# A row softmax on one core: the loads of tiles two to six issued from GpSimd, each DMA engine's share in one packet

## The chip, the core and the metric

The kernel runs on one core of a Trainium2 chip. A core has engines that each follow their own list of instructions: VectorE (DVE), ScalarE (ACT), GpSimd (POOL), SyncE (SP) and TensorE, which this kernel doesn't use. Data moves between the chip's main memory (HBM) and the core's on-chip memory (SBUF, 128 partitions) by 16 DMA engines. An engine of the core issues a transfer into a DMA queue; the DMA engines carry it out. The metric is the time of one execution on the device in microseconds, lower being better.

## What is computed

The input has 16 x 1024 = 16,384 rows of 512 float32 values, 33.55 MB; the output has the same size. Each row gets a softmax at temperature 0.5:

```python
x_scaled = x / 0.5
x_max = np.max(x_scaled, axis=-1, keepdims=True)
exp_x = np.exp(x_scaled - x_max)
return exp_x / np.sum(exp_x, axis=-1, keepdims=True)
```

## The kernel before

The 16,384 rows are cut into 8 tiles of 2048 rows, 4 MiB each. In a tile every partition holds 16 rows that lie side by side in HBM, so it gets 32 KB in one contiguous piece. There are six buffers: tiles one to six (c = 0 to 5 in the code) have one each, and tiles seven and eight take those of tiles one and two again once these are stored. All work is done in place in the buffer.

A tile is worked on in blocks of rows. The first tile has blocks of 4, 4 and 8 rows, the last has two of 8, all others are one block of 16. Its loads are cut too: the first tile arrives as two transfers, of 4 rows (8 KB in a partition, 1 MiB in all) and of 12 rows (24 KB, 3 MiB); each other tile is one transfer.

For a block, `shift` (line 68) takes each row's negated maximum on VectorE (line 74) and doubles it to a bias (line 78). `exponentials` (line 80) runs one ScalarE instruction for each row, exp(2x + bias), which sums the row as it goes (line 85). `scale_vector` (line 95) forms reciprocals (line 100) and multiplies seven eighths of the rows by them on VectorE (line 102); `scale_scalar` (line 106) does the rest on ScalarE (line 111). `store` (line 115) sends a whole tile out from ScalarE's queue after its last block (line 119).

The order is written by hand, at lines 123 to 133: the maximum of block i + 2 comes after the scaling of block i, and the exponentials of block i + 1 ahead of it. So VectorE's list takes the tiles strictly in their order, and no later tile's work can go ahead of an earlier tile's. The loads are issued by `load` (line 59), which `shift` calls at the first touch of a tile; all are issued on Sync (line 66). Sync does nothing else. The first six tiles' loads wait for nothing, as their buffers are new; the seventh's waits, among others, for the first tile's store, and the eighth's for the second's. All loads therefore stand in one queue, in the order of the tiles.

Of the kernel before, what the change touches and what calls it, by code (L numbers as in the profile page):

```python
# [1 line left out]

# [4 lines left out]


@with_exitstack
def kernel(  # L10
    ctx: ExitStack,
    tc: tile.TileContext,
    x: bass.AP,
    out: bass.AP,
):
    nc = tc.nc
    fp32 = mybir.dt.float32
    P = nc.NUM_PARTITIONS
    AX = mybir.AxisListType.X
    EXP = mybir.ActivationFunctionType.Exp  # L20
    COPY = mybir.ActivationFunctionType.Copy
    MAX = mybir.AluOpType.max

    D = x.shape[-1]
    xf = x.flatten_outer_dims()
    of = out.flatten_outer_dims()
    N = xf.shape[0]

    G = 16
    C = N // (P * G)
    assert C * P * G == N
    xr = xf.rearrange("(c p g) d -> c p g d", p=P, g=G)
    outr = of.rearrange("(c p g) d -> c p g d", p=P, g=G)
    WHOLE = [(0, G)]
    LOADS = [[(0, 4), (4, G)]] + [WHOLE] * 7
    BLOCKS = [[(0, 4), (4, 8), (8, G)]] + [WHOLE] * 6 + [[(0, 8), (8, G)]]
    STORES = [WHOLE] * 8  # L40
    BMAX = 16
    BUFS = 6

    data = ctx.enter_context(tc.tile_pool(name="data", bufs=BUFS))
    stats = ctx.enter_context(tc.tile_pool(name="stats", bufs=6))

    ctx.enter_context(tc.manual_schedule())


    warm = stats.tile([P, 1], fp32, name="warm", bufs=1)  # L50
    nc.vector.memset(warm, 0.0)  # L51
    nc.scalar.activation(out=warm, in_=warm, func=EXP)  # L52

    chunks = {}
    blocks = [(c, lo, hi) for c in range(C) for lo, hi in BLOCKS[c]]
    n = len(blocks)
    biases, sums, recips = {}, {}, {}

    def load(c):
        if c < BUFS:  # L60
            chunks[c] = data.tile([P, G, D], fp32, name="xt")
        else:
            chunks[c] = chunks[c - BUFS]
        xt = chunks[c]
        for lo, hi in LOADS[c]:
            nc.sync.dma_start(out=xt[:, lo:hi, :], in_=xr[c][:, lo:hi, :])  # L66

    def shift(i):
        c, lo, hi = blocks[i]
        if c not in chunks:  # L70
            load(c)
        b = hi - lo
        negmax = stats.tile([P, BMAX], fp32, name="negmax")
        nc.vector.tensor_reduce(  # L74
            negmax[:, 0:b], chunks[c][:, lo:hi, :], axis=AX, op=MAX, negate=True
        )
        biases[i] = stats.tile([P, BMAX], fp32, name="bias")
        nc.vector.tensor_scalar_mul(biases[i][:, 0:b], negmax[:, 0:b], 2.0)  # L78

    def exponentials(i):  # L80
        c, lo, hi = blocks[i]
        sums[i] = stats.tile([P, BMAX], fp32, name="sums")
        for g in range(hi - lo):
            row = chunks[c][:, lo + g, :]
            nc.scalar.activation(  # L85
                out=row,
                in_=row,
                func=EXP,
                bias=biases[i][:, g : g + 1],
                scale=2.0,  # L90
                accum_out=sums[i][:, g : g + 1],
            )


    def scale_vector(i):
        c, lo, hi = blocks[i]
        b = hi - lo
        k = b - b // 8
        recips[i] = stats.tile([P, BMAX], fp32, name="recip")
        nc.vector.reciprocal(recips[i][:, 0:b], sums[i][:, 0:b])  # L100
        rows = chunks[c][:, lo : lo + k, :]
        nc.vector.tensor_mul(  # L102
            rows, rows, recips[i][:, 0:k].unsqueeze(2).broadcast_to((P, k, D))
        )

    def scale_scalar(i):
        c, lo, hi = blocks[i]
        b = hi - lo
        for g in range(b - b // 8, b):
            row = chunks[c][:, lo + g, :]  # L110
            nc.scalar.activation(  # L111
                out=row, in_=row, func=COPY, scale=recips[i][:, g : g + 1]
            )

    def store(i):
        c, _, end = blocks[i]
        for lo, hi in STORES[c]:
            if hi == end:
                nc.scalar.dma_start(
                    out=outr[c][:, lo:hi, :], in_=chunks[c][:, lo:hi, :]  # L120
                )

    shift(0)
    shift(1)
    exponentials(0)
    for i in range(n):
        if i + 1 < n:
            exponentials(i + 1)
        scale_vector(i)
        scale_scalar(i)  # L130
        if i + 2 < n:
            shift(i + 2)
        store(i)


# [1 line left out]
_INS = ['x']  # L137
_OUTS = [((16, 1024, 512), 'float32')]


# [23 lines left out]
```

## Time and profile before

| What | Value |
|---|---|
| Time, median of 3 runs | 162.28 us (162.20 to 162.33) |
| The profiled execution: its time / its span | 162.34 us / 160.6 us |
| VectorE busy | 134.6 us, 84% of the span |
| ScalarE busy | 102.1 us, 64% |
| GpSimd busy | 0.2 us, four small fills at the start |
| Bytes moved | 67.13 MB, 418 GB/s over the span |
| Landing of a load after its issue | 4.9 us (first piece), 11.7 us (second piece), 30.2 us (median of the whole tiles) |
| Landing of a store after its issue | 12.2 us shortest, 22.8 us median |

The span is the time from the first to the last thing that the profile records; the time of the execution has 1.7 us around it. A landing counts from the issue, so a load that stands behind others in its queue has their transfer in its own figure. The page's strip of DMA activity, 40 slices of the span, says how full the 16 DMA engines were:

```profile
DMA  5999999999999999999999999999999999999993
GB/s 182 471 400 506 400 400 498 408 392 484 424 400 384 400 457 449 400 441 465 400 424 473 408 408 492 400 392 498 416 392 490 424 392 457 457 392 449 465 392 139
```

Each digit is the busy share in tenths, 9 for 90% or more. The row of VectorE on the page looks much the same from the fourth slice to the 37th: both resources are nearly full through the middle of the run.

### The profile page before, as it was taken

The page shows a single profiled execution, that of the slowest core. Times are in us where ns is not written, and L with a number is a line of the kernel's source. Part 1 is how long each engine was busy: PE and PEld are TensorE (multiplying, and loading weights), DVE is VectorE, ACT ScalarE, POOL GpSimd, SP SyncE. Part 2 cuts the span into 40 slices and gives each one's busy share as a digit, 9 for nine tenths or more (in the row PEclk, how much of TensorE's full clock was granted, in tenths as well). Part 3 has the DMA queues.
Part 4 walks back from the last instruction along what each step waited for, and adds up shares of the span by engine and source line. Part 5 has one row for each costly group of instructions (what it writes and reads, how often), then busy time and mean ns, then how long its engine had stood idle before and what let it go on. Part 6 is the DMA issues. An engine that isn't in the chain of part 4 may idle for free.

```text
span 160.6 us, 402 instructions
## 1 busy us (share of the span) xinstructions
DVE 134.6 (84%) x45; ACT 102.1 (64%) x273; POOL 0.2 (0%) x4
## 2 busy tenths in 40 slices
DVE  0507999999999999999999999999999999957000
ACT  3071549069979963998199909991899891790000
POOL 0000000000000000000000000000000000000000
DMA  5999999999999999999999999999999999999993
GB/s 182 471 400 506 400 400 498 408 392 484 424 400 384 400 457 449 400 441 465 400 424 473 408 408 492 400 392 498 416 392 490 424 392 457 457 392 449 465 392 139
DMA packets 2450, 67.13 MB, mean 418 GB/s; under 512 B 272, under 2 KB 272, under 8 KB 272
## 3 DMA queue, kind: packets, MB, share of 16 engines
q1 hardware_dynamic: 1296, 33.56, 49.3%
q10 hardware_dynamic: 1152, 33.55, 48.4%
q14 instruction: 2, 0.02, 0.0%
HBM read 33.55 MB, written 33.55 MB: 418 GB/s over the span
## 4 chain that ended last, share of the span: by engine, by line
DVE 80%; DMA 7%; ACT 4%; issue 0%; SPq 0%
DVE negmax L74 42%; DVE xt L102 36%; DMA xt<-in_x_dram 7%; ACT xt L85 4%; DVE bias L78 1%; DVE recip L100 1%; SPq L66 0%
## 5 line engine op out<-in xcount | busy, mean ns | idle before, releaser
L85 ACT ACTIVATE xt<-xt,bias 128x512 f32<-128x512 f32 x128 | 90.4, 708 | 41.7 <-DVE bias L78 41.2
L74 DVE TENSOR_REDUCE negmax<-xt 128x16 f32<-128x8192 f32 (+2 forms) x11 | 69.9, 6352 | 9.5 <-DMA xt<-in_x_dram 9.5
L102 DVE TENSOR_TENSOR xt<-xt,recip 128x7168 f32<-128x7168 f32 (+2 forms) x11 | 62.0, 5637 | 0.4
L85 ACT ACTIVATION_READ_ACCUMULATOR xt<-xt,bias 128x1 f32 x128 | 23.9, 187 | 0.0
L111 ACT ACTIVATE xt<-xt,recip 128x512 f32<-128x512 f32 x15 | 9.9, 706 | 0.0
L100 DVE RECIPROCAL recip<-sums 128x16 f32<-128x16 f32 (+2 forms) x11 | 2.4, 218 | 1.8 <-ACT xt L85 1.8
L78 DVE TENSOR_SCALAR bias<-negmax 128x16 f32<-128x16 f32 (+2 forms) x11 | 1.9, 173 | 0.4
L52 ACT ACT_TABLE_LOAD x1 | 1.3, 1283 | 0.7 <-PEq L148 0.7
L51 DVE MEMSET warm<- 128x1 f32 x1 | 0.1, 59 | 0.8 <-PEq L148 0.8
L52 ACT ACTIVATE warm<-warm 128x1 f32<-128x1 f32 x1 | 0.2, 203 | 0.0
L148 POOL MEMSET const-bfloat16-1.0<- 128x1 bf16 x1 | 0.1, 103 | 0.0
L148 POOL MEMSET const-uint8-127<- 128x1 uint8 x1 | 0.1, 103 | 0.0
L148 POOL MEMSET const-float32-1.0<- 128x1 f32 x1 | 0.1, 100 | 0.0
L148 POOL MEMSET const-float32-0.0<- 128x1 f32 x1 | 0.1, 99 | 0.2 <-issue 0.2
## 6 DMA issues: line engine op xcount, KB each, us to landing
out_dram<-xt ACTq DMA_DIRECT2D x8, 4096.0 KB, 22.8
xt<-in_x_dram SPq DMA_DIRECT2D x7, 4096.0 KB, 30.2
xt<-in_x_dram SPq DMA_DIRECT2D x1, 3072.0 KB, 11.7
xt<-in_x_dram SPq DMA_DIRECT2D x1, 1024.0 KB, 4.9
```

What stands on the lines that cost most here:

```text
L51: nc.vector.memset(warm, 0.0)
L52: nc.scalar.activation(out=warm, in_=warm, func=EXP)
L74: nc.vector.tensor_reduce(negmax[:, 0:b], chunks[c][:, lo:hi, :], axis=AX, op=MAX, negate=True)
L78: nc.vector.tensor_scalar_mul(biases[i][:, 0:b], negmax[:, 0:b], 2.0)
L85: nc.scalar.activation(out=row, in_=row, func=EXP, bias=biases[i][:, g : g + 1], scale=2.0, accum_out=sums[i][:, g : g + 1],)
L100: nc.vector.reciprocal(recips[i][:, 0:b], sums[i][:, 0:b])
L102: nc.vector.tensor_mul(rows, rows, recips[i][:, 0:k].unsqueeze(2).broadcast_to((P, k, D)))
L111: nc.scalar.activation(out=row, in_=row, func=COPY, scale=recips[i][:, g : g + 1])
L148: nc = _bacc.Bacc("TRN2", target_bir_lowering=False, num_devices=1)
```

## The change

Loads of tiles two to six, those with 0 < c < 6, are issued on GpSimd. A transfer is handed to the DMA engines as descriptors, records of which bytes to move, here one for each 32 KB piece; packets are what the DMA engines work through. The argument single_packet asks that what one DMA engine has of a transfer, here 8 pieces of 32 KB, be put into one packet. The two transfers of the first tile and the loads of tiles seven and eight stay on Sync. In the changed code Sync's list is four loads, GpSimd's five; the lists of VectorE and ScalarE are the same as before.

```diff
         for lo, hi in LOADS[c]:
-            nc.sync.dma_start(out=xt[:, lo:hi, :], in_=xr[c][:, lo:hi, :])
+
+            if 0 < c < BUFS:
+                nc.gpsimd.dma_start(
+                    out=xt[:, lo:hi, :], in_=xr[c][:, lo:hi, :], single_packet=True
+                )
+            else:
+                nc.sync.dma_start(out=xt[:, lo:hi, :], in_=xr[c][:, lo:hi, :])
```

## The prediction

> **What bounds the kernel now.** I read the chain of waits first, because it says whether the loads or the arithmetic set the end. Its columns are start in us, length in us, and what.
>
> ```profile
> by line: DVE negmax L74 41.7%; DVE xt L102 36.2%; DMA xt<-in_x_dram 7.3%; ACT xt L85 3.6%; DVE bias L78 1.1%; DVE recip L100 0.9%; issue 0.4%; SPq L66 0.2%
> 1.15 11.71 DMA xt<-in_x_dram
> 12.86 0.02 issue
> 12.88 2.30 DVE negmax L74
> ...
> 143.59 3.89 DVE xt L102
> ```
>
> The chain has one DMA piece, the load of rows 4 to 15 of the first tile, landing at 12.86. From 12.88 VectorE is the chain up to 147.5, but for 5.76 us of ScalarE near the end. So the rest of the span hangs on that landing: 160.6 - 12.86 = 147.7 us follow it whatever happens ahead.
>
> Next, the list of waits, to see where VectorE starves:
>
> ```profile
> DVE negmax L74 <- DMA xt<-in_x_dram: 9.5, 2, 4.8
> ```
>
> It waited for loads twice only, for the two pieces of the first tile. Tiles two to eight were always there in time. The load of the second tile is needed only at 24.63.
>
> Then the table of busy time by stretch (length, VectorE, ScalarE, GpSimd, clock, DMA share, GB/s):
>
> ```profile
> 2.50:5.60 3.10, 0.00 (x0) 0.00 (x0) 0.00 (x0) 1.00 1.01 423
> 5.60:12.90 7.30, 2.48 (x3) 2.93 (x8) 0.00 (x0) 1.00 1.03 446
> 12.90:45.60 32.70, 32.49 (x13) 20.68 (x57) 0.00 (x0) 1.00 1.00 433
> 45.60:59.00 13.40, 13.33 (x5) 12.61 (x34) 0.00 (x0) 1.00 1.01 411
> ```
>
> The DMA engines are full from 2.5 us on, during the first tile's load too: bytes put ahead of that tile delay it one for one. Between 12.9 and 45.6 only loads move, at 433 GB/s, or 27.06 GB/s for each of 16 engines. I price all loads with this.
>
> Last, the DMA view of the time in which loads (q1) and the first store (q10) compete, 46 to 69 us:
>
> ```profile
> q1 hardware_dynamic: 186, 5.57, 59.5%
> q10 hardware_dynamic: 144, 4.19, 42.2%
> ```
>
> Shares of packet time add to 101.7%: an engine serves one packet at a time, and the two queues take turns. With 32 KB in each packet, 5.57 MB are 170 packets and 4.19 MB are 128, so the load queue got 1.33 packets for one of the store queue.
>
> **What the Trainium skill says.** In "DMA: Bandwidth & Descriptors", section "Queues, rings and completion order", each DMA engine goes round its queues at packet granularity: it "drains a whole packet" from one before it switches. The turns above agree, but no run here yet shows a packet with several descriptors. The section "SWDGE vs HWDGE vs iDMA" of that page prefers packets of up to 4096 B and at most 64 descriptors, and calls the packet the context-switching boundary; GpSimd's queue and Sync's are different queues of an engine. The section "The descriptor swizzle" counts eight data descriptors and one completion for each engine of a 128-partition transfer; the page's 1296 packets of the load queue are 9 loads x 16 engines x 9, in agreement. In "Latency and other measured facts" the first byte takes about 0.6 us from Sync and about 1 us from GpSimd. The trace has the first Sync issue at 0.73 and packets from about 1.7 us; GpSimd's figure no run here shows.
>
> **The change part by part.** Order and number of instructions on VectorE and ScalarE are unchanged. Sync loses five load issues, GpSimd gains five, and nothing on GpSimd waits ahead of them.
>
> 1. Removed from Sync: five issues of 0.42 to 0.65 us. In the trace they follow the two issues of the first tile and nobody waits for their issue time, so the gain is nothing. The loads of the seventh and eighth tile wait for stores in any case (56.4 us the longest wait on Sync), and nothing stands between them that the change moves.
>
> 2. Added on GpSimd: five issues, on an engine idle after 0.43 us. It isn't shown how long one takes. By the skill's 1 us the first tile-2 descriptors are at the DMA engines near 0.7 + 1 = 1.7 us (an estimate); I take 2.5 us, and bound it by 1.7 and, for a slow start, 7 us. VectorE is idle up to 5.61, so it can't be in the way of the first ones. By 2.5 us Sync's queue has moved 19 packets, about one for each engine, of the 16 data packets (8 of 8 KB, 8 of 24 KB) an engine has for the first tile.
>
> 3. The packets. In each GpSimd load an engine has 8 x 32 KB = 262,144 B, and with single_packet that is one packet. At 27.06 GB/s a share holds the engine for 262,144 / 27.06e3 = 9.69 us. Sync's packets of the first tile hold it for 0.31 or 0.91 us. Taking turns then means: a Sync packet or 1.33, a share of 9.69 us, a Sync packet or 1.33, the next share, and so on. Before, the first tile stood ahead of all others in one queue; now all five are ahead of most of it. There are five shares, and five turns let through only 5 x 1.33 = 6.7 of about 15 Sync packets. So all five shares go by before the last Sync packet, on every engine. This holds for any start of GpSimd up to when 6.7 Sync packets are left: 12.86 - 6.7 x 0.91 = 6.8 us.
>
> 4. The cost. The second piece of the first tile lands later by 5 x 9.69 = 48.4 us, at 61.3 instead of 12.86. What hides it? Nothing: VectorE has only the first block (2.29 + 0.17 us) to do before, and the second tile, although landed early, comes after the first in VectorE's order. The first piece (8 KB packets) is late as well, by up to five shares, but lands some 7 us (8 packets of 0.91) ahead of the second, which covers its 2.46 us on VectorE and four exponentials on ScalarE.
>
> 5. Afterwards. All of tiles one to six are in place when VectorE starts, so its 134.6 us run as before. The first store goes out at 45.58 + 48.4 = 94.0 with no load beside it; it took 23.7 us in competition and 12.2 alone (the shortest landing of a store). Tile seven's load can start near 106 and is needed at 103.94 + 48.4 = 152.3: no new wait. The DMA engines have more idle time later, which buys nothing, since VectorE doesn't wait there. The last store lands as before, about 12.2 us after its issue.
>
> 6. A GpSimd queue to close at the end may add a little: between 0 and about 0.5 us, an estimate by the size of one issue; I take 0.
>
> Sum: the profiled execution took 162.34 us, of which the span is 160.6 and 1.7 lie around it. 160.6 + 48.4 = 209.0 of span, 210.7 us in all; its own time stands 0.06 above the median of 162.28, so against the median it is the same. I write 210.5.
>
> In general the time is 162.3 + 9.69 k, where k is the number of GpSimd shares (or their equal in bytes) that pass before the last Sync packet of the first tile. The rivals are values of k.
>
> **Rivals.**
> - Turns by descriptor: the DMA engine switches after each 32 KB, as it does between loads and stores. Then about 14 Sync packets at 1.33 to 1 let 10.5 to 14 descriptors of 1.21 us in between: 12.7 to 17 us, so 175 to 179 us. For it speaks that each descriptor of 32 KB is one packet of the record before; against it, that the change asks for one packet.
> - Only a few shares ahead: the engine already holds most of the first tile's packets when GpSimd's arrive, or shares bandwidth by bytes. One share is 172.0, equal bytes (240 KB, 8.9 us) 171.2, three shares 191. For it: Sync issues both pieces by 1.6 us. Against it: the two queues of before do take turns while both have work queued long before.
> - The other side: GpSimd's first descriptors reach the DMA engines only after the first tile has gone, at 12.86 or later. Then the queue order is that of before, tile two has until 24.63, and the time is 162.3; with less traffic behind it the first tile might land up to 0.5 us earlier (4.19 MB at 433 GB/s are 9.7 us from 1.7, that is 11.4, plus the slow start), so 161.8 to 162.5. It would need 12 us between barrier and first packet on an otherwise idle engine; nothing in the profile speaks for so much. Beyond 12.86 + about 2 us tile two would itself be late, which is slower again.
>
> **How the numbers follow.** All five shares ahead: 0.55, from 205 to 214 (the loads at 411 GB/s, the rate of 45.6 to 59, would make 51.0 us of the 48.4, so 213.3). By descriptor: 0.17. A few shares or equal bytes: 0.11. GpSimd late: 0.13, of it 0.09 no change and 0.04 faster. Still slower than 214, by GpSimd loads that run below the rate of Sync's: 0.04. Differences within 0.2% (0.3 us) count as none. The range from 171 to 214 takes in the first three; the likeliest case alone has 205 to 214. Slower is 0.55 + 0.17 + 0.11 + 0.04 = 0.87.
>
> **What would show it.** Right: VectorE's wait for loads grows from 9.5 to about 58 us, the chain's DMA piece ends near 61, GpSimd's queue moves 20.97 MB nearly all before the first tile's last packet, and from there the chain repeats that of before shifted by 48 us. By-descriptor turns would put the landing at 25 to 30 and a mix of both queues in that time. A first GpSimd packet after 12.9, with the landing at 12.86, would make the forecast wrong altogether; a landing in between gives k. If VectorE waits for loads again after the first tile, step 5 is wrong.

## The result, and the profile after

The changed kernel takes 171.26 us (median of 4 runs, 171.25 to 171.29), the kernel before 162.24: a ratio of 1.0556, 95% interval 1.0538 to 1.0575. It is 9 us slower. The forecast was slower too, but by 48 us. Of all the runs in this document one is left out of the comparisons, because it took over 1.5% longer than the fastest of its kernel: 192.97 us of e3_desc8k_no_single.

The chain of waits after (start in us, length, what), to be held against the one of before:

```profile
by line: DVE negmax L80 39.5%; DVE xt L108 34.3%; DMA xt<-in_x_dram 12.6%; ACT xt L91 3.4%; DVE bias L84 1.0%; DVE recip L106 0.9%; issue 0.4%; SPq L72 0.2%
...
1.16 21.35 DMA xt<-in_x_dram
22.54 2.30 DVE negmax L80
...
153.25 3.89 DVE xt L108
```

The shape is that of before. The one DMA piece, the second piece of the first tile, ends at 1.16 + 21.35 = 22.51 instead of 12.86, 9.65 us later, and VectorE's last instruction starts at 153.25 instead of 143.59, 9.66 us later. Everything between is carried along unchanged. The list of waits says the same, and shows no new wait:

```profile
DVE negmax L80 <- DMA xt<-in_x_dram: 19.2, 2, 14.5
```

VectorE waits for loads twice, as before, for 19.2 us instead of 9.5.

So the place was as forecast, and the size was not. The DMA view of the stretch from 6.8 to 21.6 us shows why (queue, packets, MB, share of the 16 engines; q0 is GpSimd's queue, q1 Sync's):

```profile
DMA packets 224, 6.42 MB, mean 434 GB/s; under 512 B 0, under 2 KB 0, under 8 KB 0
## 3 DMA queue, kind: packets, MB, share of 16 engines
q0 software_dynamic: 112, 3.67, 57.4%
q1 hardware_dynamic: 112, 2.75, 43.1%
```

112 and 112: seven from each queue on each of 16 engines, one of 32 KB from GpSimd and one of 24 KB from Sync in turn. A share, the eight descriptors that one DMA engine has of a load, does not go through as a unit. The record counts each descriptor as a packet on GpSimd's queue as well, although the transfer was issued with single_packet.

Where GpSimd begins is seen in the list by time (start, length, engine, line, in brackets the idle time before) and in the DMA view from 1.2 to 5.55 us. The list:

```profile
1.24 2.75 POOL L68 DMA_DIRECT2D xt<-in_x_dram  x5 [0.79 <-PEq L165]
```

The DMA view of that stretch has one queue:

```profile
q1 hardware_dynamic: 160, 1.44, 88.8%
```

GpSimd has issued all five loads by 4.0, but up to 5.55 only Sync's queue moves data. GpSimd's first 16 descriptors start between 5.59 and 6.10. By then each engine has moved the first piece and one packet of the second, which is why the first piece still lands in 4.8 us. What is left on each engine is seven packets and the small write that reports completion. Each of these eight lets one descriptor by. The DMA view from 5 to 21.62 us, when the first completions of the second piece are written, counts them:

```profile
q0 software_dynamic: 128, 4.19, 58.4%
```

128 on 16 engines are 8 on each. By the packets' recorded durations one takes 1.213 us; 8 x 1.213 = 9.70 us, against 9.65 measured.

The span grew by 8.9 us, not 9.65. Before, the last store took 12.16 us to land, since the preceding store still had data in the queue (164 packets in the last 13.1 us, where one store is 144). Now it lands in 11.13 us. The end of the span follows the landing by 1.13 us instead of 0.85, which takes 0.28 of this back.

### The profile page after: what moved, and what is told of

It reads as the page before. It is cut to its first block, busy times and chain, and to the rows that moved or that the text cites. A ratio compares the mean times of both kernels' runs of the same rounds, so it can differ in the third digit from the quotient of the medians.

```text
span 169.5 us, 404 instructions
## 1 busy us (share of the span) xinstructions
DVE 134.6 (79%) x45; ACT 102.3 (60%) x273; POOL 3.0 (2%) x9
## 4 chain that ended last, share of the span: by engine, by line
DVE 76%; DMA 13%; ACT 3%; issue 0%; SPq 0%
DVE negmax L80 40%; DVE xt L108 34%; DMA xt<-in_x_dram 13%; ACT xt L91 3%; DVE bias L84 1%; DVE recip L106 1%; SPq L72 0%
## 5 line engine op out<-in xcount | busy, mean ns | idle before, releaser
L80 DVE TENSOR_REDUCE negmax<-xt 128x16 f32<-128x8192 f32 (+2 forms) x11 | 69.9, 6353 | 19.2 <-DMA xt<-in_x_dram 19.2
L68 POOL DMA_DIRECT2D xt<-in_x_dram x5 | 2.8, 557 | 0.8 <-PEq L165 0.8
## 6 DMA issues: line engine op xcount, KB each, us to landing
xt<-in_x_dram POOLq DMA_DIRECT2D x5, 4096.0 KB, 39.5
```

The costliest lines, as they stand in the source:

```text
L68: nc.gpsimd.dma_start(out=xt[:, lo:hi, :], in_=xr[c][:, lo:hi, :], single_packet=True)
L80: nc.vector.tensor_reduce(negmax[:, 0:b], chunks[c][:, lo:hi, :], axis=AX, op=MAX, negate=True)
```

## The experiments

Theory T: a DMA engine that has work in several queues takes one descriptor from each in turn, whatever single_packet says. A transfer with n descriptors left on an engine is therefore delayed by n times the length of the other queue's descriptor. The main rivals were that a whole share, but only one, gets ahead (9.69 us, the same size by chance); that turns are equal in bytes; that GpSimd's path has a price of its own; and that the price is in proportion to what is moved to GpSimd. All diffs are against the changed kernel unless something else is said.

**Without the argument (e1_no_single)**

```diff
-                    out=xt[:, lo:hi, :], in_=xr[c][:, lo:hi, :], single_packet=True
+                    out=xt[:, lo:hi, :], in_=xr[c][:, lo:hi, :]
```

> The changed kernel without single_packet. Theory T (a DMA engine changes queues after every descriptor, whatever packet it belongs to): nothing changes, 171.3 us within 0.3, the second piece of the first tile lands at 22.5 again. Rival R (the argument does shape the turns, and only about one share got ahead): without it the turns should be other than now, with a landing clearly before or after 22.5 and a time at least 1 us away from 171.3.

Measured: 171.28 us, landing at 22.47. For descriptors of 32 KB the argument makes no difference.

**Short descriptors on GpSimd (e2_desc8k, e3_desc8k_no_single)**

```diff
-                    out=xt[:, lo:hi, :], in_=xr[c][:, lo:hi, :], single_packet=True
+                    out=xt[:, lo:hi, :], in_=xr[c][:, lo:hi, :], single_packet=True,
+                    max_dma_last_dim=8192
```

The second of the two has max_dma_last_dim in place of single_packet.

> The changed kernel with GpSimd's descriptors cut from 32 KB to 8 KB, still single_packet, so a share is 32 descriptors in one packet. Theory T: each of the 8 turns given to GpSimd now costs 0.31 us instead of 1.21, so the delay is about 8 x 0.31 = 2.5 us and the time 164 to 165. Rivals: one whole share ahead of Sync's packets, or turns equal in bytes, leave the delay at 8 to 9.7 us, 170 to 171.5.

> As e2_desc8k but without single_packet. Theory T: the same as e2_desc8k within 0.3 us. Rival R: the two differ by more than 1 us, since 32 descriptors to a packet or 1 is then a large difference.

Measured: 191.65 us and, for the three runs of e3_desc8k_no_single that are compared, 189.05 us. The time is far from every expectation, but the landing is T's. The chain of waits of e2_desc8k:

```profile
1.15 14.31 DMA xt<-in_x_dram
15.48 2.30 DVE negmax L81
...
90.01 27.31 another core or an unknown queue
117.34 8.70 DVE negmax L81
```

The second piece lands at 15.46, 2.60 us later than before; T said 2.5. One share ahead, or turns equal in bytes, would have been 8 to 9.7. What follows is a wait that no theory had: VectorE stands still for 27.31 us until 117.34. The chain can't name it; the list of waits puts it down to a load ("DVE negmax L81 <- DMA xt<-in_x_dram: 39.5, 3, 27.3"), and it is the sixth tile's, GpSimd's last. The DMA view from 70 to 110 us explains it:

```profile
q1 hardware_dynamic: 252, 7.73, 44.9%
q10 hardware_dynamic: 257, 7.37, 42.7%
q0 software_dynamic: 259, 2.11, 12.5%
```

Three queues, Sync's loads of tiles seven and eight (q1), the stores (q10) and GpSimd's loads (q0), get the same number of packets, 252 to 259. With 32 KB in those of the first two and 8 KB in GpSimd's, GpSimd's loads have an eighth of the engines. Short descriptors made them harmless to the first tile, and then starved the sixth, by the same rule.

The two kernels are not equal, as T had it within 0.3 us. The four runs of e2_desc8k lie between 191.31 and 193.41, the three of e3_desc8k_no_single between 188.95 and 190.00; their medians are 2.6 us apart, more than the 1 us that rival R asked for. It is weak evidence for R all the same. The first tile lands alike in both, at 15.46 and 15.35, and from 70 to 110 us the three queues get equal counts without single_packet too (255, 256 and 260). In that stretch a DMA engine gets to one of GpSimd's descriptors about every 2.5 us (259 on 16 engines in 40 us). So one descriptor more or less on the slowest engine is worth about 2.5 us (an estimate). In the profiled runs, 1.6 us apart, the difference is one descriptor: of GpSimd's 2560 the last starts at 115.45 in e2_desc8k, the last but one at 113.94, and the last of e3_desc8k_no_single at 113.85. The runs of e2_desc8k alone lie 2.1 us apart. What makes the one descriptor late stays open; the next pair has no such stretch and asks the question again.

**Short descriptors on the stores too (e10_all8k, e11_all8k_no_single)**, to test the explanation of the long wait:

```diff
-                    out=xt[:, lo:hi, :], in_=xr[c][:, lo:hi, :], single_packet=True
+                    out=xt[:, lo:hi, :], in_=xr[c][:, lo:hi, :], single_packet=True, max_dma_last_dim=8192
...
-                    out=outr[c][:, lo:hi, :], in_=chunks[c][:, lo:hi, :]
+                    out=outr[c][:, lo:hi, :], in_=chunks[c][:, lo:hi, :],
+                    max_dma_last_dim=8192,
```

> As e2_desc8k, with the stores cut into descriptors of 8 KB too. Theory T: the landing of the first tile's second piece stays at 15.5, and in turns with stores of 8 KB the loads no longer fall behind, so VectorE's 27 us wait for the sixth tile goes: 164 to 166 us. Rival (8 KB descriptors are slow on the GpSimd path in themselves): still near 190.

> As e10_all8k without single_packet. Theory T: the same as e10_all8k within 0.5 us. Rival R (single_packet shapes turns): more than 1 us apart from it.

Measured: 164.49 and 164.37 us, within 0.12 of each other, so single_packet makes no difference here with 32 descriptors in a share either. The long wait is gone: 12.0 us for loads in all, 9.5 before plus the 2.5 of the first tile. From 52 to 72 us the two queues take turns at equal counts and, now, equal bytes:

```profile
q10 hardware_dynamic: 546, 4.34, 51.2%
q0 software_dynamic: 540, 4.22, 49.8%
```

**Only the sixth tile on GpSimd (e4_only_tile6)**

```diff
-            if 0 < c < BUFS:
+            if c == BUFS - 1:
```

> Only the load of the sixth tile goes through GpSimd; tiles two to five are back on Sync. Theory T: eight descriptors for each engine are enough to stand between the first tile's packets, so 171.3 us again within 0.5, landing at 22.5, and no other load late. Rival (the cost is in proportion to what is moved to GpSimd): a fifth of the 9 us, 164.

Measured: 171.05 us, landing at 22.49. A fifth of the bytes costs all of the 9 us. What counts is how many turns pass before the first tile is in, and eight descriptors an engine fill them all. The load that now overtakes isn't needed before the sixth tile.

**The same loads on ScalarE's queue (e5_scalar_queue, against the kernel before)**

```diff
-    warm = stats.tile([P, 1], fp32, name="warm", bufs=1)
-    nc.vector.memset(warm, 0.0)
-    nc.scalar.activation(out=warm, in_=warm, func=EXP)
...
-            nc.sync.dma_start(out=xt[:, lo:hi, :], in_=xr[c][:, lo:hi, :])
+            eng = nc.scalar if 0 < c < BUFS else nc.sync
+            eng.dma_start(out=xt[:, lo:hi, :], in_=xr[c][:, lo:hi, :])
...
+    for c in range(BUFS):
+        load(c)
+    warm = stats.tile([P, 1], fp32, name="warm", bufs=1)
+    nc.vector.memset(warm, 0.0)
+    nc.scalar.activation(out=warm, in_=warm, func=EXP)
```

> Loads of tiles two to six on ScalarE's queue, issued at the start of its list (ahead of the table load), none on GpSimd. Theory T: turns between queues, not GpSimd, cost the time; this queue starts as early as Sync's, so all 16 packets of the first tile on an engine each let one 32 KB descriptor by: 16 x 1.21 = 19.4 us, about 181 us; the first piece lands near 14 and the second near 32. Rival (GpSimd's software path is what costs): 162.3.

Measured: 180.76 us. The chain's DMA piece:

```profile
1.14 31.21 DMA xt<-in_x_dram
```

The second piece lands at 32.35, 19.49 us later than before; 16 x 1.213 = 19.4. No GpSimd takes part, and it is worse than with GpSimd, because this queue's first descriptors start at 2.45 to 3.10 us, after one packet of the first tile instead of nine. It is the second queue that costs, not who writes to it.

**GpSimd held back (e6_gate_piece1, e7_gate_piece2)**

```diff
+    load(0)
+    gate = stats.tile([P, 1], fp32, name="gate", bufs=1)
+    nc.gpsimd.tensor_copy(out=gate, in_=chunks[0][:, 0, 0:1])
+    for c in range(1, BUFS):
+        load(c)
     shift(0)
     shift(1)
```

e7_gate_piece2 copies from row 4 instead of row 0.

> As the changed kernel, but GpSimd first copies one element of the first tile's first piece, so its loads start only after that piece landed (5.6). If the first GpSimd data follows 3.5 to 4.4 us behind its first issue as now, it comes at 9.3 to 10.2 and 2 to 4 packets of the first tile are left. Theory T: 2 to 4 turns x 1.21 us, less some 0.7 at the end: 164 to 166.5. Rival (a share that goes as a whole, or a fixed price of the GpSimd path): 171.

> As e6_gate_piece1, but the copied element is of the second piece, so GpSimd's loads start after 12.9. Theory T: the second piece lands at 12.9 as before; the second tile's data starts near 17, lands near 27 and is needed at 24.6, so VectorE waits some 2 to 3 us there: 164 to 166. Rival (fixed price of the GpSimd path): 171.

Measured for e6_gate_piece1: 166.36 us. By the packets' times one engine starts its first GpSimd descriptor at 9.52, with three packets and the completion left; the other 15 start theirs from 10.16 to 10.70, with two packets left. The landing waits for the slowest engine: 4 x 1.213 = 4.9 us, landing 17.49, 4.63 later than before.

Measured for e7_gate_piece2: 165.90 us. The first tile lands as before, the second tile at 25.7. From the list by time:

```profile
13.08 2.74 POOL L68 DMA_DIRECT2D xt<-in_x_dram  x5
...
25.76 8.69 DVE L80 TENSOR_REDUCE negmax<-xt 128x16 f32<-128x8192 f32 x1 [0.92 <-DMA xt<-in_x_dram]
```

The number was met, and its reason only in part. VectorE is late by 1.1 us (25.76 against 24.63), not 2 to 3, and its last store is issued at 148.69 instead of 147.55. The span is longer by 3.6 us all the same. The DMA engines stood empty from the end of the first tile, about 12.6, to the first GpSimd data at 14.4 to 15.2, and the first descriptors after that took 2.0 us (median of 16) instead of 1.21. From the last store's issue to the end of the span are 15.5 us instead of 13.0. The DMA engines are full up to that issue (length, VectorE, ScalarE, GpSimd, clock, DMA share, GB/s):

```profile
126.00:148.00 22.00, 20.04 (x10) 14.55 (x37) 0.00 (x0) 1.00 1.00 430
```

So the stores ahead of the last one aren't gone when it is issued. The DMA engines had no slack to lose.

**Short descriptors on Sync (e8_sync8k)**

```diff
                 nc.sync.dma_start(
                     out=xt[:, lo:hi, :], in_=xr[c][:, lo:hi, :],
+                    max_dma_last_dim=8192 if c == 0 else 32768,
                 )
```

> The changed kernel with the first tile's second piece cut into descriptors of 8 KB on Sync, 24 for each engine instead of 8. Theory T: about 21 of them are left when GpSimd's first arrives, each lets one 32 KB descriptor by, 21 x 1.21 = 25.4 us: about 187 us, landing near 38. Rivals: one share ahead, or turns equal in bytes: 171 as now.

Measured: 187.74 us, landing at 39.58. The same bytes in three times as many descriptors are delayed by 26.7 us, that is 22 x 1.213. From 6 to 38 us:

```profile
q0 software_dynamic: 367, 10.98, 79.6%
q1 hardware_dynamic: 366, 2.88, 21.3%
```

Equal counts again, at 3.8 times the bytes. This rules out turns by bytes and a single share ahead, which both said 171.

**The first tile in three pieces, all on Sync (e9_split, against the kernel before)**

```diff
-    LOADS = [[(0, 4), (4, G)]] + [WHOLE] * 7
+    LOADS = [[(0, 4), (4, 8), (8, G)]] + [WHOLE] * 7
```

> The kernel before, all loads on Sync, with the first tile loaded in three pieces (rows 0 to 3, 4 to 7, 8 to 15) that match its three blocks. If the end hangs on the landing that VectorE's second block waits for, that landing moves from 12.9 to near 8 and the third piece lands at 12.9, when VectorE is just free: the chain starts 4.7 us earlier. But then the DMA engines, 67.13 MB at 433 GB/s = 155 us plus the start, bind: 158 to 160 us. Rival (the first landing is not what the end hangs on): 162.3.

Measured: 162.78 us, ratio 1.0027 (1.0012 to 1.0042) to the kernel before, a miss. VectorE's second block did start early, at 8.01 instead of 12.88, and its wait for loads fell from 9.5 to 6.8 us, of which 2.1 are a new wait for the second tile. The last store is issued at 145.54, 2.0 us sooner than before. But the span is 160.7 against 160.6. The stretches before the end, by the table of busy time:

```profile
126.00:146.00 20.00, 17.57 (x7) 11.88 (x32) 0.00 (x0) 1.00 0.99 429
146.00:160.70 14.70, 0.00 (x0) 0.00 (x0) 0.00 (x0) 1.00 0.80 346
```

The DMA engines are at 0.99 and 429 GB/s before the last store is even issued, so there are 15.2 us from its issue to the end instead of 13.0. The kernel before has the same share and rate up to its last store:

```profile
126.00:148.00 22.00, 19.58 (x7) 13.90 (x36) 0.00 (x0) 1.00 0.99 429
```

It is held at about 160 us twice over, by VectorE and by the DMA engines. Being late costs; being 2 us early brought nothing. No version that beats it came out of these runs.

## Why the prediction was wrong

In the table, the turns are the data descriptors of the other queue that an engine has done when the completion of the first tile's second piece is written; where engines differ, on the slowest. The delay is that of the landing of the second piece against the 12.86 us of before.

| Run | Turns on each engine | Length of one, us | Product | Delay, us | Time, us |
|---|---|---|---|---|---|
| e2_desc8k | 8 | 0.31 | 2.5 | 2.60 | 191.65 |
| e6_gate_piece1 | 4 | 1.213 | 4.9 | 4.63 | 166.36 |
| changed kernel | 8 | 1.213 | 9.7 | 9.65 | 171.26 |
| e5_scalar_queue | 16 | 1.213 | 19.4 | 19.49 | 180.76 |
| e8_sync8k | 22 | 1.213 | 26.7 | 26.72 | 187.74 |

Step 1 (nothing gained on Sync): right; the first tile's issue and first data are where they were, and no wait moved.

Step 2 (GpSimd's first data at 2.5 us, bounds 1.7 to 7): within the bounds and taken wrongly; it was 5.6. By itself this would not have mattered for the forecast, which held for any start up to 6.8.

Step 3 is the step that failed: "In each GpSimd load an engine has 8 x 32 KB = 262,144 B, and with single_packet that is one packet", and the turn that follows from it, 9.69 us. The turn was one descriptor, 1.21 us. I had read in the Trainium skill, "DMA: Bandwidth & Descriptors", section "Queues, rings and completion order", that an engine drains a whole packet before it switches, and took it that the argument makes the packet. The measurement decides: with or without the argument the engines switched after each descriptor, of 32 KB as of 8 KB. Since the record counts each descriptor as a packet, the page's rule, to switch after a packet, isn't contradicted; that the argument makes one packet of eight descriptors is. Whether a packet exists that holds an engine longer isn't shown by any run here. The same page's preference for packets of up to 4096 B, in the section "SWDGE vs HWDGE vs iDMA", was quoted in the forecast, and was a reason to doubt a packet of 262,144 B.

The 1.33 Sync packets to a turn in step 3 were misread as well. The window of 46 to 69 us begins before the first store has data, at 49.64. From there on the two queues of the kernel before are even (DMA view, 49.6 to 69 us):

```profile
q1 hardware_dynamic: 144, 4.19, 50.1%
q10 hardware_dynamic: 144, 4.19, 50.1%
```

Step 4 (nothing hides the delay, it reaches the end one for one): right, 9.65 at the landing and 9.66 at VectorE's last instruction. The formula's 5 x 9.69 fell with step 3. That the first piece would be late as well was wrong in the changed kernel, for the start of step 2, and right in e5_scalar_queue, where it landed 14.6 us after its issue.

Step 5 (no new wait, the last store as before): right on waits; the store landed 1.0 us sooner, since the 12.2 us of before, which the forecast took for a store alone, had been behind another store. Step 6 took 0 for the closing of a queue; the end of the span came 0.28 us later after the last landing, within its bounds. The other runs bear on this: the last landing is followed by 0.85 to 0.91 us where GpSimd issues no load (before, e5_scalar_queue, e9_split), by 0.88 with one load (e4_only_tile6) and by 1.12 to 1.14 in every run with five. So the use of GpSimd's queue alone doesn't cost it; why five loads do stays open.

The rival "turns by descriptor" had the mechanism and was given 0.17. Its 175 to 179 us came from a start at 2.5 and from the 1.33; e5_scalar_queue, which started that early, had 16 turns and not 10.5 to 14. With the start at 5.6 it is 8 x 1.21 = 9.7, so 162.3 + 9.7 - 0.75 = 171.3, where 0.75 is what the end of the span gained. That one share (172.0) and equal bytes (171.2; 240 KB are 9.1 us and not 8.9, so 171.4) come to the same time is chance: e2_desc8k and e8_sync8k rule both out. What should have weighed more was the view above, of loads against stores before: two queues taking turns of one descriptor each. That was evidence on the engine, where the argument was only a word in the code.

## What to carry to other kernels

Loads in one queue arrive in the order in which they are needed; spread over two queues they arrive in turns, descriptor by descriptor, and the urgent one pays one foreign descriptor for each of its own. Where transfers must share the engines, the size of a descriptor is the weight: long descriptors on the urgent queue and short ones on the other are a priority, and they remain one when the roles change, as e2_desc8k shows. Before speeding up one of two full resources, check the other: e9_split freed VectorE by two microseconds, and the DMA engines took them.

## What the runs showed that was not expected

A queue that joins busy DMA engines starts late. GpSimd's first data came 1.4 to 2.2 us after its first issue where the engines were empty (e7_gate_piece2: issue at 13.08, the first 16 descriptors from 14.44 to 15.24); the forecast's step 2 had about 1 us. Where Sync's queue was running, it took 4.4 to 4.9 us in the changed kernel and 3.8 to 4.9 in e6_gate_piece1. It isn't GpSimd alone: in the kernel before, the first store, from ScalarE's queue, is issued at 45.58 and its first 16 descriptors start at 49.64 to 50.82, 4.1 to 5.2 us later. In e8_sync8k the first store, issued at 72.30, finds the engines empty, and its first 16 start at 73.18 to 73.34, 0.9 to 1.0 us later. So a running queue costs a newcomer about 3 us or more (an estimate from these differences); what holds it back was not tried. In the changed kernel this delay is worth a good deal: where the second queue starts with the first, as in e5_scalar_queue, the cost is twice as high.
